# Second block's projections with the tokens' high and low parts side by side in one 512-column product

## The chip, the cores and the metric

One core of one Trainium2 chip runs the kernel. The metric is the device time of an execution in microseconds (us): the median of several runs, 1727.61 us for the kernel before (three runs, 1727.26 to 1727.88). The engines are TensorE (PE, with its weight loads as PEld), VectorE (DVE), ScalarE (ACT), GpSimd (POOL) and SyncE (SP), which issues the DMAs.

## The reference, cut to what matters

Two transformer blocks run one after the other on 256 tokens of width 1024 in float32; the first one has a mixture of experts. The change touches only the second:

```python
def second_block(x, ...):
    h = x + 0.5 * swiglu(rmsnorm(x, ffn1_norm), w_gate1, w_up1, w_down1)      # D_FF = 2816
    n = rmsnorm(h, mix_norm)
    z = n @ w_in                                                              # 1024 -> 2560
    q, k, v = z[..., :512], z[..., 512:1024], z[..., 1024:1536]
    attn = moba_attention(q, k, v)
    zg = gelu(z[..., 1536:])
    gm = chunked_spatial_gating(zg[..., :512], zg[..., 512:], ...)
    gates = sigmoid(n @ w_gate + b_gate)                                      # 1024 -> 2048
    merged = gates[..., :1024] * (attn @ w_branch_attn) + gates[..., 1024:] * (gm @ w_branch_gmlp)
    h = h + merged @ w_out
    h = h + 0.5 * swiglu(rmsnorm(h, ffn2_norm), w_gate2, w_up2, w_down2)
    return rmsnorm(h, final_norm)

def swiglu(x, w_gate, w_up, w_down):
    return (silu(x @ w_gate) * (x @ w_up)) @ w_down
```

## The kernel before

Activations lie transposed: 128 features on the partitions, the T = 256 tokens along the free axis, KD = 8 such chunks for the width of 1024. To reach float32 precision, every operand of a projection is split into a high part (a copy rounded to fp32r, made by ScalarE) and a low part (the rest, a subtraction by VectorE). `mm3` (L307 to L312) then issues three products per chunk k of the contracted width: high weights by high tokens, high weights by low tokens, low weights by high tokens, each a matmul of 128 x 128 weights with 256 token columns, all summed in one half of a PSUM bank. `xn.pair` is the pair of token tiles (`nhi`, `nlo`) that class `Normed` (L494 on) fills.

The weights come in "units" of 128 x 1024 (class `Units`): `uh` is the high part (ScalarE, L434), `ul` the low part (VectorE, L448). A unit is used by one group of 24 matmuls. `U.get(i)` emits the low part of unit i + 2 first (AHEAD = 2) and the high part of one more, so the `ul` instructions stand in VectorE's queue where the code asks for units. The program's order on each engine is the order in which the code issues; an engine runs its queue in that order.

The second block has these stages, named by their PSUM tile:

- **gu and dn** of the first FFN: `swiglu` runs over f = 0 to 21 (128 of the 2816 hidden features each). Per f it issues a gate group and an up group (8 chunks, 24 matmuls each) into the two halves of one bank; then VectorE multiplies the bank by the row scale `rs` (L1145), and `act` goes on with sigmoid (ScalarE), two multiplications (L1149, L1152) and the split (L302, L303). The down product of an earlier f (`dn`, L405, 24 matmuls of 256 columns) follows. L1199 and L509 at the end make the new residual `x` and the normed `nlo`.
- **z**: 10 column blocks j of w_in in two groups each. When `rs` is known, the groups' bank is read: q is copied by ScalarE, k is scaled by VectorE, v is copied by ScalarE (`values2`, tile `vt2`) and turned by TensorE, the rest goes through `gelu2`.
- **gt**: the gates, 8 blocks of two groups; between the groups stand steps of the attention and of the spatial gating (`pipe.tick`). VectorE scales (L1931), ScalarE takes a tanh (L1934). The attention's last step (`PT`, `pvo`) closes the stage.
- **br**: 8 chunks c; per c two groups of 4 chunks k with `ath`/`atl` and `gmh`/`gml` as tokens into two halves of one bank. `merged` combines them with the gates: L1946 (a scalar_tensor_tensor that reads the bank), L1947, a copy by ScalarE into `mgh`, and L1951 for `mgl`.
- **o**: 8 groups with `mgh`/`mgl`; one scalar_tensor_tensor per group adds the result to the residual.
- **gu and dn** of the second FFN, as before, but its down products (L2005) hold tokens as the stationary side and stream 512 columns of weights.

The working tiles in PSUM come from pool `psV` (four banks, `wps`).

Of the kernel before, what the change touches and what calls it, by code (L numbers as in the profile page):

```python
# [20 lines left out]
T = 256  # L21
# [25 lines left out]
def body(ctx: ExitStack, tc: tile.TileContext, I, out, dbg=None, n_experts=NE):  # L47
# [258 lines left out]
    def mm3(ps, wl, xl, nk, first=True, k0=0):  # L306
        (wh, wo), (xh, xo) = wl, xl  # L307
        for k in range(nk):
            for a, b in ((wh(k), xh[:, k0 + k, :]), (wh(k), xo[:, k0 + k, :]), (wo(k), xh[:, k0 + k, :])):
                nc.tensor.matmul(ps, a, b, start=first, stop=False, skip_group_check=True)  # L310
                first = False

    def rsqrt(pool, v, n, name):

        h = pool.tile([128, n], I32, name=name + "h", tag=name + "h", bufs=1)
        y = pool.tile([128, n], F32, name=name, tag=name, bufs=2)
        a = pool.tile([128, n], F32, name=name + "a", tag=name + "a", bufs=1)
# [175 lines left out]
    class Normed:  # L493


        def __init__(self, pool, x, gain):
            self.x, self.gain = x, gain
            self.hi = pool.tile([128, KD, T], F32R, name="nhi", tag="nhi", bufs=1)
            self.lo = pool.tile([128, KD, T], F32R, name="nlo", tag="nlo", bufs=1)
            self.pair = (self.hi, self.lo)  # L500

# [630 lines left out]
    def swiglu(F, n, xn, seq, down, each=None, y=None):  # L1132


        sp = {}
        gups = {}
        st = Stats(B, acc) if y is None else Rstd(B, acc, y)
        rs = None

        def act(f, halves=((0, 2),)):  # L1140
            gu = F.tile([128, 2, T], F32, name="gu", tag="gu", bufs=2)
            s = F.tile([128, T], F32, name="fs", tag="fs", bufs=2)
            for a0, a1 in halves:
                p = gups[f][a0][:, a0 * T:a1 * T].rearrange("p (a t) -> p a t", t=T)
                nc.vector.tensor_tensor(gu[:, a0:a1, :], p,  # L1145
                                        rs[:, None, :].to_broadcast([128, a1 - a0, T]), op=OP.mult)
                if a0 == 0:
                    nc.scalar.activation(s, gu[:, 0, :], AF.Sigmoid)  # L1148
                    nc.vector.tensor_tensor(s, gu[:, 0, :], s, op=OP.mult)  # L1149
                if a1 == 1:  # L1150
                    yield
# [4 lines left out]
        for kind, f in seq:  # L1156
            if kind == "gu":
                last = f == NF - 1
                gups[f] = [wps("gu")] * 2
                if last:  # L1160
                    gups[f] = gups[f][0], wps("gu")
                mm3(gups[f][0][:, 0:T], pair(U.get(order[("g", n, f)])), xn.pair, KD)
                if f == 0 and y is None:
# [607 lines left out]
    with ExitStack() as mx:  # L1771
        Q = mx.enter_context(tc.tile_pool(name="mix2", bufs=1, side="right"))
        ath = Q.tile([128, 4, T], F32R, name="ath")
        atl = Q.tile([128, 4, T], F32R, name="atl")
        gmh = Q.tile([128, 4, T], F32R, name="gmh")
        gml = Q.tile([128, 4, T], F32R, name="gml")

# [34 lines left out]

        def gelu2(ps, rs, dst, j):

            z = W3.tile([128, 2, T], F32, name="z", tag="z", bufs=2)
            t = W3.tile([128, 2, T], F32, name="ge", tag="ge", bufs=2)
            nc.vector.tensor_tensor(z, ps, rs[:, None, :].to_broadcast([128, 2, T]), op=OP.mult)
            nc.scalar.activation(t, z, AF.Square)
# [9 lines left out]

        def values2(ps, dst):
            d = W3.tile([128, 2, T], F32, name="vt2", tag="vt2", bufs=1)  # L1830
            nc.scalar.activation(d, ps, AF.Copy)
            yield
            yield from turned(d, dst, st.r.y)
# [50 lines left out]
        for n, j in enumerate(IN2):  # L1884
            ps = wps("z2")
            for a in range(2):
                mm3(ps[:, a * T:(a + 1) * T], pair(U.get(order[("in2", j, a)])), xn.pair, KD, first=(a == 0))
                pipe.tick()
# [8 lines left out]
                elif 2 * n + a == 2:  # L1897
# [3 lines left out]
                    nc.gpsimd.dma_start(ws, I["gmlp_w_s_2"][0].rearrange("g i j -> i g j"))  # L1901
            held.append((j, ps.rearrange("p (a t) -> p a t", a=2)))
            while rs is not None and held:
                k, z = held.pop(0)
                i = 2 * (k % 2)
                if k < 2:
                    nc.scalar.activation(q2[:, i:i + 2, :], z, AF.Copy)
                elif k < 4:
                    nc.vector.tensor_tensor(k2[:, i:i + 2, :], z, rs[:, None, :].to_broadcast([128, 2, T]), op=OP.mult)
                elif k < 6:  # L1910
                    pipe.start(values2(z, v2[:, :, i * 128:(i + 2) * 128]))
                else:
                    pipe.start(gelu2(z, rs, None if k < 8 else vg[:, :, i * 128:(i + 2) * 128], i))
# [6 lines left out]
        for j in range(8):  # L1920
            ps = wps("gt")
            for a in range(2):
                mm3(ps[:, a * T:(a + 1) * T], pair(U.get(order[("gate", j, a)])), xn.pair, KD, first=(a == 0))
                pipe.tick()
# [3 lines left out]
                if c in (2, 5, 8, 11):  # L1928
                    pipe.start(A.step(c // 3))
            g = gts[:, 2 * j % 8:2 * j % 8 + 2, j // 4, :]  # L1930
            nc.vector.tensor_tensor(g, ps.rearrange("p (a t) -> p a t", a=2), rs[:, None, :].to_broadcast([128, 2, T]),  # L1931
                                    op=OP.mult)
# [7 lines left out]
        W = mx.enter_context(tc.tile_pool(name="mix2d", bufs=1, side="right"))  # L1940
        mgh = W.tile([128, KD, T], F32R, name="mgh")
        mgl = W.tile([128, KD, T], F32R, name="mgl")

        def merged(c, ps):
            g = gts[:, c]
            nc.vector.scalar_tensor_tensor(g, g, 1.0, ps.rearrange("p (a t) -> p a t", a=2), op0=OP.add, op1=OP.mult)  # L1946
            nc.vector.tensor_tensor(g[:, 0, :], g[:, 0, :], g[:, 1, :], op=OP.add)  # L1947
# [5 lines left out]
        for j in range(2):  # L1953
            for a in range(2):
                ua, ug = (U.get(order[(s, j, a)]) for s in ("ba", "bg"))
                for o in range(2):
                    ps = wps("br")
                    mm3(ps[:, 0:T], pair(ua, 256, o * 128), (ath, atl), 4)
                    mm3(ps[:, T:2 * T], pair(ug, 256, o * 128), (gmh, gml), 4, first=False)
                    pipe.tick()  # L1960
# [126 lines left out]
```

## Time and profile before

| | us |
|---|---|
| median of three runs | 1727.61 |
| the profiled execution | 1726.06 |
| its span in the trace | 1724.3 |
| TensorE busy | 1606.3 |
| VectorE busy | 679.9 |
| ScalarE busy | 520.0 |
| second block, first FFN's first group to the end | about 1159 to 1724.3 |

The span is the time from the first to the last instruction of the profiled execution; the execution itself is 1.76 us longer. Busy times are the sum of an engine's instructions with overlaps taken out. A matmul's own duration in the trace (0.28 us for 256 columns) is longer than its step, the time from its start to the next one's, since matmuls overlap; where TensorE runs without a stop, the step is the time that counts, and it is read from a stretch of the chain or of the timeline divided by its matmuls.

### The profile page before, as it was taken

Reading aid. Unit: us, or ns where it says so; the run is one execution under the profiler, and the core shown is the slowest. Engines: PE = TensorE matmul, PEld = TensorE weight load, DVE = VectorE, ACT = ScalarE, POOL = GpSimd, SP = SyncE. Lnnn points to the kernel's source line nnn. Section 1 sums busy time; section 2 is a strip of 40 time slices with the busy share of each in tenths; the row PEclk is TensorE's granted clock in tenths of the full one; section 3 lists DMA queues with packets and bytes.
Section 4 is the critical chain, followed back from the end, with each engine's and each line's share of the span. In section 5 each row is a group of like instructions: output and inputs, shape, how many; then the busy total and the mean of one; then the engine's idle time right before and its main releaser. Section 6 shows DMA issues by size and latency. Waiting matters only on the chain. (4 is left out here: it accounts for less than half of the span.)

```text
span 1724.3 us, 25602 instructions
## 1 busy us (share of the span) xinstructions
PE 1606.3 (93%) x10067; PEld 982.3 (57%) x10067; DVE 679.9 (39%) x1428; ACT 520.0 (30%) x983; POOL 21.9 (1%) x39
## 2 busy tenths in 40 slices
PE   6999899999999799999999889879999999999997
PEld 3776333333333233333333233249999999999997
DVE  4656412122121212212121212146666765666666
ACT  2544312111011101201111111044444547554443
POOL 1000000000000000000000000100000000000000
PEclk7999999999999999999999999989999999999999
DMA  9987899899999999999999999965555653545652
GB/s 329 357 284 297 348 415 414 328 414 413 417 413 415 413 413 416 415 416 415 413 416 412 413 415 411 415 244 181 178 189 178 201 171 123 165 159 178 197 170 98
DMA packets 169756, 545.69 MB, mean 316 GB/s; under 512 B 11281, under 2 KB 90721, under 8 KB 133729
## 3 DMA queue, kind: packets, MB, share of 16 engines
q1 hardware_dynamic: 168304, 540.60, 81.6%
q8 instruction: 130, 2.13, 0.5%
q0 software_dynamic: 480, 1.58, 0.3%
q10 hardware_dynamic: 784, 0.92, 0.2%
q14 instruction: 58, 0.47, 0.1%
HBM read 542.01 MB, written 1.05 MB: 315 GB/s over the span
## 5 line engine op out<-in xcount | busy, mean ns | idle before, releaser
L1597 PE MATMUL u<-chunk,xg 128*64 128x512 f32 x2048 | 475.8, 604 | 16.7 <-DMA chunk<-in_w_mlp_dram 13.9
L1597 PEld LDWEIGHTS u<-chunk,xg 128*64 128x64 f32 x2048 | 152.7, 138 | 275.9 <-issue 235.6
L448 DVE TENSOR_TENSOR ul<-chunk,uh 128x1024 fp32r<-128x1024 f32 x202 | 239.2, 1220 | 36.3 <-ACT uh L434 34.9
L1499 PE MATMUL yp<-chunk,aT 128*64 128x512 f32 x1024 | 235.8, 602 | 9.5 <-ACT aT L1484 8.1
L434 ACT ACTIVATE uh<-chunk 128x1024 fp32r<-128x1024 f32 x202 | 205.1, 1050 | 58.4 <-DMA chunk<-in_ffn_w_up_dram 24.1
L310 PE MATMUL gu<-nhi,uh 128*128 128x256 f32 x704 | 200.0, 284 | 0.0
L310 PE MATMUL gu<-nhi,ul 128*128 128x256 f32 x704 | 199.4, 283 | 0.0
L310 PE MATMUL gu<-nlo,uh 128*128 128x256 f32 x704 | 199.4, 283 | 0.0
L1499 PEld LDWEIGHTS yp<-chunk,aT 128*64 128x64 f32 x1024 | 68.0, 137 | 128.3 <-issue 113.8
L310 PEld LDWEIGHTS gu<-nhi,uh 128*128 128x128 f32 x704 | 135.3, 192 | 1.2 <-issue 0.4
L310 PEld LDWEIGHTS gu<-nlo,uh 128*128 128x128 f32 x704 | 135.3, 192 | 0.9
L310 PEld LDWEIGHTS gu<-nhi,ul 128*128 128x128 f32 x704 | 135.3, 192 | 0.0
L1474 DVE TENSOR_SCALAR g<-u 128x256 f32<-128x256 f32 x64 | 27.1, 423 | 226.3 <-PE u L1597 222.9
L1509 DVE SCALAR_TENSOR_TENSOR yl<-yp,tg,yh 128x512 fp32r<-128x512 f32 x32 | 24.0, 751 | 222.9 <-ACTq L1627 172.2
L1475 ACT ACTIVATE s<-g 128x256 f32<-128x256 f32 x66 | 27.2, 413 | 234.8 <-DVE g L1474 232.2
L1508 ACT ACTIVATE yh<-yp,tg 128x512 fp32r<-128x512 f32 x32 | 22.0, 687 | 165.4 <-PEq L1696 148.7
L1484 ACT ACTIVATE aT<-apt 128x256 f32<-128x256 f32 x64 | 24.5, 383 | 141.6 <-PE apt L297 74.2
L1253 ACT ACTIVATE xr<-xrp,yg 128x512 f32<-128x512 f32 x32 | 22.0, 688 | 146.3 <-PE xrp L1242 146.3
L1145 DVE TENSOR_TENSOR gu<-gu,rs 128x512 f32<-128x512 f32 (+1 forms) x46 | 30.7, 668 | 80.7 <-PE gu L310 80.2
L1271 DVE TENSOR_TENSOR xg<-xrp,gs 128x128 f32<-128x128 f32 x64 | 18.7, 292 | 106.8 <-ACT xg L1266 106.8
L1266 ACT ACTIVATE xg<-xrp,modT,gs 128x64 f32<-128x64 f32 x128 | 44.8, 400 | 51.2 <-PE xrp L1260 39.7
L1148 ACT ACTIVATE fs<-gu 128x256 f32<-128x256 f32 x44 | 18.4, 418 | 122.9 <-DVE gu L1145 122.9
(472 smaller groups left out, 2362.8 us busy)
## 6 DMA issues: line engine op xcount, KB each, us to landing
chunk<-in_w_mlp_dram SPq DMA_DIRECT2D x384, 1024.0 KB, 19.9
chunk<-in_w_ada_dram SPq DMA_DIRECT2D x24, 1024.0 KB, 7.3
chunk<-in_ffn_w_gate_dram SPq DMA_DIRECT2D x22, 1024.0 KB, 5.6
chunk<-in_ffn_w_up_dram SPq DMA_DIRECT2D x22, 1024.0 KB, 8.0
chunk<-in_ffn_w_down_dram SPq DMA_DIRECT2D x22, 1024.0 KB, 5.8
chunk<-in_w_in_dram SPq DMA_DIRECT2D x17, 1024.0 KB, 5.2
chunk<-in_w_gate_dram SPq DMA_DIRECT2D x8, 1024.0 KB, 5.4
chunk<-in_w_out_dram SPq DMA_DIRECT2D x6, 1024.0 KB, 8.0
```

What stands on the lines that cost most here:

```text
L310: nc.tensor.matmul(ps, a, b, start=first, stop=False, skip_group_check=True)
L434: nc.scalar.activation(hi if spec is None else spec(hi), view(raw(key)), AF.Copy)
L448: nc.vector.tensor_tensor(vl, view(raw(key)), vh.bitcast(F32), op=OP.subtract)
L1145: nc.vector.tensor_tensor(gu[:, a0:a1, :], p, rs[:, None, :].to_broadcast([128, a1 - a0, T]), op=OP.mult)
L1253: nc.scalar.activation(xr[q][0:w, :], ps[1 + q][0:w, :], AF.Copy, scale=ps[0][0:w, :])
L1266: nc.scalar.activation(xg[:, k, :], at, AF.Identity, scale=gs[:, 2, k:k + 1], bias=modT[:, 24 + k:25 + k])
L1474: nc.vector.tensor_scalar(g, uv[:, :, 0], 7.0, None, op0=OP.min)
L1475: nc.scalar.activation(s, g, AF.Sigmoid, scale=1.702)
L1484: nc.scalar.activation(aT[:, r * 256:(r + 1) * 256], pt[:, r * 256:(r + 1) * 256], AF.Copy)
L1499: nc.tensor.matmul(yp[w * d:w * d + w, 0:m], a, wt[:, o:o + m], start=(q + h == 0), stop=(q + h == 4), skip_group_check=True, tile_positio ...
L1509: nc.vector.scalar_tensor_tensor(yl, yp[:, 0:m], tg[:, 1:2], yh.bitcast(F32), op0=OP.mult, op1=OP.subtract)
L1597: nc.tensor.matmul(u, xg[j][:, k, :], raw(("m1", e, k))[:, n * 512:(n + 1) * 512], start=False, stop=(k == KD - 1), skip_group_check=True, ...
```

## The change

A helper `wide3` takes the place of `mm3` in all projections of the second block except the down products. Per chunk k it issues two matmuls instead of three: the high weights with 512 columns (256 high and 256 low tokens, which now lie side by side in one tile), and the low weights with the 256 high tokens. The 512 columns fill a whole PSUM bank, whose halves have to be added: `summed` is a VectorE tensor_reduce over pairs (256 outputs from 512 inputs whose partners lie 256 elements apart). Each group now takes a bank of its own, and the steps that read PSUM before read the summed tile in SBUF. In o the two halves are added by two scalar_tensor_tensor. The ScalarE copies of q and v out of PSUM fall away, as the sums write q2 and `vt2` themselves.

```diff
+    def wide3(ps, wl, both, nk, first=True):
+        wh, wo = wl
+        for k in range(nk):
+            nc.tensor.matmul(ps, wh(k), both[:, k], start=first, stop=False, skip_group_check=True)
+            nc.tensor.matmul(ps[:, 0:T], wo(k), both[:, k, 0, :], start=False, stop=False, skip_group_check=True)
+            first = False
+    def summed(dst, ps):
+        nc.vector.tensor_reduce(dst, ps.rearrange("p (s t) -> p t s", s=2), axis=AX.X, op=OP.add)
...
-            self.hi = pool.tile([128, KD, T], F32R, name="nhi", tag="nhi", bufs=1)
-            self.lo = pool.tile([128, KD, T], F32R, name="nlo", tag="nlo", bufs=1)
-            self.pair = (self.hi, self.lo)
+            self.both = pool.tile([128, KD, 2, T], F32R, name="nboth", tag="nboth", bufs=1)
+            self.hi, self.lo = self.both[:, :, 0, :], self.both[:, :, 1, :]
...
-                gups[f] = [wps("gu")] * 2
-                if last:
-                    gups[f] = gups[f][0], wps("gu")
-                mm3(gups[f][0][:, 0:T], pair(U.get(order[("g", n, f)])), xn.pair, KD)
+                gus[f] = F.tile([128, 2, T], F32, name="gu", tag="gu", bufs=2)
+                ps = [wps("gu") for _ in range(2)]
+                wide3(ps[0], pair(U.get(order[("g", n, f)])), xn.both, KD)
+                summed(gus[f][:, 0, :], ps[0])
...
-                mm3(gups[f][1][:, T:2 * T], pair(U.get(order[("u", n, f)])), xn.pair, KD, first=last)
+                wide3(ps[1], pair(U.get(order[("u", n, f)])), xn.both, KD)
+                summed(gus[f][:, 1, :], ps[1])
...
-        def values2(ps, dst):
-            d = W3.tile([128, 2, T], F32, name="vt2", tag="vt2", bufs=1)
-            nc.scalar.activation(d, ps, AF.Copy)
+        def values2(d, dst):
...
-            ps = wps("z2")
+            i = 2 * (j % 2)
+            if j < 4:
+                z = (q2, k2)[j // 2][:, i:i + 2, :]
+            else:
+                z = W3.tile([128, 2, T], F32, name="z", tag="vt2" if j < 6 else "z", bufs=1 if j < 6 else 2)
             for a in range(2):
-                mm3(ps[:, a * T:(a + 1) * T], pair(U.get(order[("in2", j, a)])), xn.pair, KD, first=(a == 0))
+                ps = wps("z2")
+                wide3(ps, pair(U.get(order[("in2", j, a)])), xn.both, KD)
+                summed(z[:, a, :], ps)
...
-            ps = wps("gt")
+            g = gts[:, 2 * j % 8:2 * j % 8 + 2, j // 4, :]
             for a in range(2):
-                mm3(ps[:, a * T:(a + 1) * T], pair(U.get(order[("gate", j, a)])), xn.pair, KD, first=(a == 0))
+                ps = wps("gt")
+                wide3(ps, pair(U.get(order[("gate", j, a)])), xn.both, KD)
+                summed(g[:, a, :], ps)
...
+            t = W.tile([128, 2, T], F32, name="brs", tag="brs", bufs=2)
+            for a in range(2):
+                summed(t[:, a, :], ps[a])
+            nc.vector.scalar_tensor_tensor(g, g, 1.0, t, op0=OP.add, op1=OP.mult)
...
-                    ps = wps("br")
-                    mm3(ps[:, 0:T], pair(ua, 256, o * 128), (ath, atl), 4)
-                    mm3(ps[:, T:2 * T], pair(ug, 256, o * 128), (gmh, gml), 4, first=False)
+                    ps = [wps("br") for _ in range(2)]
+                    wide3(ps[0], pair(ua, 256, o * 128), atb, 4)
+                    wide3(ps[1], pair(ug, 256, o * 128), gmb, 4)
...
-                mm3(ps[:, :T], pair(U.get(order[("out2", j, a)])), (mgh, mgl), KD)
-                nc.vector.scalar_tensor_tensor(x4[:, c, :], ps[:, :T], 0.5, x3[:, c, :], op0=OP.mult, op1=OP.add)
+                wide3(ps, pair(U.get(order[("out2", j, a)])), mgb, KD)
+                for p, x in ((ps[:, 0:T], x3), (ps[:, T:2 * T], x4)):
+                    nc.vector.scalar_tensor_tensor(x4[:, c, :], p, 0.5, x[:, c, :], op0=OP.mult, op1=OP.add)
```

The scheduling is that of the code, so what moves is VectorE's queue. In the middle of the first FFN, VectorE's rows for one f before (operation, output<-inputs, size; L1145 is the multiplication by `rs`):

```order
L1145 TENSOR_TENSOR gu<-gu,rs 128x512
L1149 TENSOR_TENSOR fs<-gu,fs 128x256
L1152 TENSOR_TENSOR fs<-gu,fs 128x256
L303 TENSOR_TENSOR spl<-fs,sph 128x256
L448 TENSOR_TENSOR ul<-chunk,uh 128x1024 x3
```

And now (L324 is the sum, L461 the low part of a unit, L1156 the multiplication):

```order
L324 TENSOR_REDUCE gu<-gu 128x256
L461 TENSOR_TENSOR ul<-chunk,uh 128x1024
L324 TENSOR_REDUCE gu<-gu 128x256
L1156 TENSOR_TENSOR gu<-gu,rs 128x512
L1160 TENSOR_TENSOR fs<-gu,fs 128x256
L1163 TENSOR_TENSOR fs<-gu,fs 128x256
L303 TENSOR_TENSOR spl<-fs,sph 128x256
L461 TENSOR_TENSOR ul<-chunk,uh 128x1024 x2
```

A sum of the gate group stands between two low parts of units, and a sum of the up group ahead of the multiplication; VectorE meets two waits for TensorE per f instead of one.

In the br stage, VectorE's rows before from a pair of low parts on (L1946, L1947 and L1951 are `merged`):

```order
L448 TENSOR_TENSOR ul<-chunk,uh 128x1024 x2
L1951 TENSOR_TENSOR mgl<-gts,mgh 128x256
L1946 SCALAR_TENSOR_TENSOR gts<-gts,br 128x512
L1947 TENSOR_TENSOR gts<-gts 128x256
L1951 TENSOR_TENSOR mgl<-gts,mgh 128x256
L1946 SCALAR_TENSOR_TENSOR gts<-gts,br 128x512
L1947 TENSOR_TENSOR gts<-gts 128x256
```

And now the same stretch (L1963, L1964 and L1968 are `merged`):

```order
L461 TENSOR_TENSOR ul<-chunk,uh 128x1024 x2
L1968 TENSOR_TENSOR mgb<-gts,mgb 128x256
L324 TENSOR_REDUCE brs<-br 128x256 x2
L1963 SCALAR_TENSOR_TENSOR gts<-gts,brs 128x512
L1964 TENSOR_TENSOR gts<-gts 128x256
L1968 TENSOR_TENSOR mgb<-gts,mgb 128x256
L324 TENSOR_REDUCE brs<-br 128x256 x2
L1963 SCALAR_TENSOR_TENSOR gts<-gts,brs 128x512
L1964 TENSOR_TENSOR gts<-gts 128x256
```

Each L1946 has got two sums ahead of it, so twelve entries stand where eight stood.

## Rows read from the trace of the kernel before

**Rows 1.** The page, busy times of the whole span.

```profile
PE 1606.3 (93%) x10067; PEld 982.3 (57%) x10067; DVE 679.9 (39%) x1428; ACT 520.0 (30%) x983; POOL 21.9 (1%) x39
```

**Rows 2.** Windows by stage: length, busy us (xinstructions) per engine, PEclk, DMA share, GB/s.

```profile
1176.00:1344.00 168.00, 168.00 (x1400) 168.00 (x1401) 105.99 (x139) 72.71 (x99) 0.00 (x0) 1.00 0.58 189
1355.00:1414.00 59.00, 59.00 (x496) 58.41 (x493) 42.03 (x71) 28.40 (x41) 2.03 (x2) 1.00 0.58 181
1414.00:1478.00 64.00, 62.56 (x529) 56.78 (x528) 33.03 (x58) 44.68 (x103) 0.00 (x0) 1.00 0.37 122
1478.00:1500.30 22.30, 22.30 (x197) 22.13 (x196) 18.95 (x29) 10.68 (x16) 0.00 (x0) 1.00 0.62 193
1500.30:1522.00 21.70, 21.70 (x194) 21.70 (x193) 16.19 (x25) 11.61 (x16) 0.00 (x0) 1.00 0.59 191
```

**Rows 3.** Chain of waits, second block: start, us, engine, tile, line, xinstructions.

```profile
1387.36 23.03 PE z L310 x192
...
1478.33 21.98 PE br L310 x192
1500.32 21.76 PE o L310 x192
...
1566.68 5.74 PE gu L310 x48
1572.41 2.80 PE dn L2005 x12
```

**Rows 4.** Timeline of TensorE in the first block's y stage: start, us, work.

```profile
147.06 0.62 PE L1039 MATMUL y<-u,mixh 128*128 128x512 f32 x2
147.51 0.39 PE L1039 MATMUL y<-u,mixl 128*128 128x512 f32 x1
147.74 0.62 PE L1039 MATMUL y<-u,mixh 128*128 128x512 f32 x2
...
150.46 0.62 PE L1039 MATMUL y<-u,mixh 128*128 128x512 f32 x2
```

**Rows 5.** VectorE groups by form: out<-in, xcount, busy, mean ns, idle before.

```profile
L1474 DVE TENSOR_SCALAR g<-u 128x256 f32<-128x256 f32 x64 | 27.1, 423 | 226.3 <-PE u L1597 222.9 <-DVEq L1678 3.0
...
L565 DVE TENSOR_REDUCE attst<-sc 128x1 f32<-128x256 f32 x16 | 6.6, 415 | 0.0
...
L935 DVE TENSOR_REDUCE ss<-scr 128x4 f32<-128x512 f32 x2 | 1.4, 682 | 0.0
...
L1447 DVE TENSOR_REDUCE gt<-og 128x32 f32<-128x128 f32 x2 | 0.7, 374 | 0.1
```

**Rows 6.** Timeline of VectorE, one f of the first FFN.

```profile
1265.28 0.69 DVE L1145 TENSOR_TENSOR gu<-gu,rs 128x512 f32<-128x512 f32 x1 [2.26 <-PE gu L310]
1266.45 0.43 DVE L1149 TENSOR_TENSOR fs<-gu,fs 128x256 f32<-128x256 f32 x1 [0.48 <-ACT fs L1148]
...
1268.16 3.49 DVE L448 TENSOR_TENSOR ul<-chunk,uh 128x1024 fp32r<-128x1024 f32 x3
1273.91 0.69 DVE L1145 TENSOR_TENSOR gu<-gu,rs 128x512 f32<-128x512 f32 x1 [2.27 <-PE gu L310]
```

**Rows 7.** Timeline of VectorE in the br stage.

```profile
1485.10 2.36 DVE L448 TENSOR_TENSOR ul<-chunk,uh 128x1024 fp32r<-128x1024 f32 x2
1487.37 0.42 DVE L1951 TENSOR_TENSOR mgl<-gts,mgh 128x256 fp32r<-128x256 f32 x1
1487.71 0.68 DVE L1946 SCALAR_TENSOR_TENSOR gts<-gts,br 128x512 f32<-128x512 f32 x1
1488.42 0.43 DVE L1947 TENSOR_TENSOR gts<-gts 128x256 f32<-128x256 f32 x1
1488.76 0.42 DVE L1951 TENSOR_TENSOR mgl<-gts,mgh 128x256 fp32r<-128x256 f32 x1
```

**Rows 8.** Windows of the in2 projections.

```profile
1386.90:1398.60 11.70, 11.70 (x101) 11.70 (x99) 9.10 (x24) 3.73 (x5) 1.09 (x1) 1.00 0.33 98
1398.60:1410.60 12.00, 12.00 (x103) 12.00 (x102) 11.57 (x15) 7.55 (x9) 0.00 (x0) 1.00 0.68 210
```

**Rows 9.** Timeline of TensorE at the first down product.

```profile
1175.94 0.39 PE L405 MATMUL dn<-sph,ul 128*128 128x256 f32 x1 [0.88 <-DVE ul L448]
```

**Rows 10.** Chain of waits at the ends of the first FFN and of gt.

```profile
1344.83 2.27 DVE ul L448 x2
1347.10 1.20 DVE x L1199 x2
...
1475.03 0.70 DVE gts L1931
```

More of the change, by code (lines that the diff above doesn't have):

```diff
@@ L1135, in swiglu @@
         sp = {}
-        gups = {}
+        gus = {}
         st = Stats(B, acc) if y is None else Rstd(B, acc, y)
@@ L1140, in act @@
         def act(f, halves=((0, 2),)):
-            gu = F.tile([128, 2, T], F32, name="gu", tag="gu", bufs=2)
+            gu = gus[f]
             s = F.tile([128, T], F32, name="fs", tag="fs", bufs=2)
             for a0, a1 in halves:
-                p = gups[f][a0][:, a0 * T:a1 * T].rearrange("p (a t) -> p a t", t=T)
-                nc.vector.tensor_tensor(gu[:, a0:a1, :], p,
+                nc.vector.tensor_tensor(gu[:, a0:a1, :], gu[:, a0:a1, :],
                                         rs[:, None, :].to_broadcast([128, a1 - a0, T]), op=OP.mult)
@@ L1772, in body @@
         Q = mx.enter_context(tc.tile_pool(name="mix2", bufs=1, side="right"))
[L1773 to L1776, printed above, removed]
+        atb = Q.tile([128, 4, 2, T], F32R, name="atb")
+        ath, atl = atb[:, :, 0, :], atb[:, :, 1, :]
+        gmb = Q.tile([128, 4, 2, T], F32R, name="gmb")
+        gmh, gml = gmb[:, :, 0, :], gmb[:, :, 1, :]
         gts = Q.tile([128, KD, 2, T], F32, name="gts")
@@ L1811, in turned, with gelu2 @@
                         nc.scalar.activation(d[:, b, :], pt[:, b * 128:(b + 1) * 128], AF.Copy, scale=scale[:, b:b + 1])
-        def gelu2(ps, rs, dst, j):
-            z = W3.tile([128, 2, T], F32, name="z", tag="z", bufs=2)
+        def gelu2(z, rs, dst, j):
             t = W3.tile([128, 2, T], F32, name="ge", tag="ge", bufs=2)
-            nc.vector.tensor_tensor(z, ps, rs[:, None, :].to_broadcast([128, 2, T]), op=OP.mult)
+            nc.vector.tensor_tensor(z, z, rs[:, None, :].to_broadcast([128, 2, T]), op=OP.mult)
             nc.scalar.activation(t, z, AF.Square)
@@ L1901, in body @@
                     nc.gpsimd.dma_start(ws, I["gmlp_w_s_2"][0].rearrange("g i j -> i g j"))
-            held.append((j, ps.rearrange("p (a t) -> p a t", a=2)))
+            held.append((j, z))
             while rs is not None and held:
@@ L1905, in body @@
                 i = 2 * (k % 2)
[L1906 to L1910, printed above, removed]
+                if 2 <= k < 4:
+                    nc.vector.tensor_tensor(z, z, rs[:, None, :].to_broadcast([128, 2, T]), op=OP.mult)
+                elif 4 <= k < 6:
                     pipe.start(values2(z, v2[:, :, i * 128:(i + 2) * 128]))
-                else:
+                elif k >= 6:
                     pipe.start(gelu2(z, rs, None if k < 8 else vg[:, :, i * 128:(i + 2) * 128], i))
@@ L1929, in body @@
                     pipe.start(A.step(c // 3))
-            g = gts[:, 2 * j % 8:2 * j % 8 + 2, j // 4, :]
-            nc.vector.tensor_tensor(g, ps.rearrange("p (a t) -> p a t", a=2), rs[:, None, :].to_broadcast([128, 2, T]),
+            nc.vector.tensor_tensor(g, g, rs[:, None, :].to_broadcast([128, 2, T]),
                                     op=OP.mult)
@@ L1940, in body @@
         W = mx.enter_context(tc.tile_pool(name="mix2d", bufs=1, side="right"))
-        mgh = W.tile([128, KD, T], F32R, name="mgh")
-        mgl = W.tile([128, KD, T], F32R, name="mgl")
+        mgb = W.tile([128, KD, 2, T], F32R, name="mgb")
+        mgh, mgl = mgb[:, :, 0, :], mgb[:, :, 1, :]
         def merged(c, ps):
             g = gts[:, c]
-            nc.vector.scalar_tensor_tensor(g, g, 1.0, ps.rearrange("p (a t) -> p a t", a=2), op0=OP.add, op1=OP.mult)
+            t = W.tile([128, 2, T], F32, name="brs", tag="brs", bufs=2)
+            for a in range(2):
+                summed(t[:, a, :], ps[a])
+            nc.vector.scalar_tensor_tensor(g, g, 1.0, t, op0=OP.add, op1=OP.mult)
             nc.vector.tensor_tensor(g[:, 0, :], g[:, 0, :], g[:, 1, :], op=OP.add)
```

## The prediction

> **What bounds the kernel now.** I read the page's busy times first: TensorE works 93% of the span, VectorE 39% [rows 1]. [...] The change takes columns' overhead from TensorE and gives VectorE 140 sums (88 in the FFNs, 20 in z, 16 in gt, 16 in br), so the question is where VectorE can't carry them.
>
> **TensorE's part.** The chain gives steps where TensorE never stops. Per matmul of 256 columns: z 23.03/192 = 120.0 ns, gu 5.74/48 = 119.6, which I round to 120, o 21.76/192 = 113.3 [rows 3]. The same shape costs two prices, by the tiles it reads. For 512 columns with 128 x 128 weights there are two prices as well: in y 15 matmuls start between 147.06 and 150.46, 3.40/15 = 226.7 ns [rows 4]; dn of the second FFN takes 2.80/12 = 233.3 [rows 3]. A k costs now 3 x 120 = 360 in gu, z and gt, and 3 x 113.3 = 340 in br and o. After: one of 512 and one of 256. The cheap 512 goes with the dear 256 as a pattern: 226.7 is 106.7 above 120, so 512 columns bear the same overhead of 13.3 as 256 do, and I pair 226.7 + 120 = 346.7 for gu, z and gt, where the moving and the stationary tiles stay what they were. That saves 13.3 ns per k. For br and o I pair 233.3 + 113.3 = 346.7, 6.7 ns more than now. Bounds: 233.3 + 120 = 353.3 (saves 6.7) and 226.7 + 113.3 = 340 (saves 20).
>
> The k's are 22 x 2 x 8 x 2 = 704 in the FFNs, 160 in z, 128 in gt, 64 in br and 64 in o. Of gu's, 48 at the start of the first FFN lie beside waits of their own and save nothing. 944 x 13.3 ns = **-12.6 us**; o adds 64 x 6.7 ns = +0.4.
>
> **What a sum costs.** No row shows a reduce over pairs out of PSUM. A plain one takes 415 ns for 256 inputs and 682 for 512 [rows 5], 1.04 ns per input, whatever leaves it. At that rate a sum is 0.68 us, 0.65 from start to start. Two things could add to it: partners 256 elements apart, and 256 outputs. Reading PSUM in steps costs nothing where the trace has it: 128x256 taken from every second element of u takes 423 [rows 5], about the 415 of a plain reduce of as many. The reduce that steps by 32 elements in SBUF, four inputs to an output, takes 374 for 128 inputs [rows 5]; half of what lies between 415 and 682 taken off 415 is 281 for 128, so it pays 93 ns more: 0.7 per input or 2.9 per output. Carried over, a sum would be 0.68 + 512 x 0.7 = 1.04 us, or 0.68 + 256 x 2.9 = 1.42. I take 0.68, since the u row reads PSUM as the sum does, and keep 1.04 and 1.42 as the ends.
>
> [...]
>
> **Where the sums are hidden, and where not.** *The FFNs.* One f lasts 1273.91 - 1265.28 = 8.63 us, of which VectorE waits 2.27 for gu, so it works 6.37 [rows 6] (less its short waits for ScalarE, which don't move). Two sums make it 7.7. TensorE's f becomes 8.64 less 16 x 13.3 ns = 8.43: the sums fit, and cost nothing while a sum stays below 1.03. PSUM doesn't stop it: four banks hold two f's, and a sum follows its group at once.
> *Start of the first FFN.* TensorE already waits 0.88 us for a `ul` at the first down product [rows 9]; sums now stand in that queue ahead of it. Two sums ahead of it, less the little slack, are +1.2, and one more at the next unit some +0.75 (estimates from 0.65 a sum): **+2.0**.
> *End of the first FFN.* The chain runs over VectorE there: ul 2.27, then x 1.20 [rows 10]. The last up group's sum stands ahead, and the gate's beside: +0.65 to +1.3, I take **+1.1**.
> *z.* From 1386.9 to 1410.6 VectorE works 9.10 of 11.7 and then 11.57 of 12.0 [rows 8]: 3.0 us idle, and eight groups' sums want 5.2. So it falls 2.2 behind, 3.1 with the 0.85 that TensorE would gain there. What it owes are units' low parts, which TensorE needs. I take **+2.6**.
> *gt.* VectorE has half its time [rows 2]. Only the last sum lies on the chain into L1931 at 1475.03 [rows 10]: **+0.7**.
> *br.* Per c VectorE does half a pair of low parts, 2.27/2, then 0.34, 0.71 and 0.34 from start to start [rows 7], 2.53 together, and about 2.56 with its small gaps; TensorE's c is 24 x 114.5 ns = 2.75 [rows 3]. Two sums make VectorE's 3.9. Eight c's are 31, from a queue that starts on the first sum some 3.1 us into the stage (a `ul` pair stands ahead, as before). I walked its queue by the order of the change: the last mgb comes 32.0 us into br, and out2's first group, whose last k needs it, ends at 32.45. Before it ended at 21.98 + 21.76/8 = 24.7. **+7.7**, the largest loss; the stage's balance gives about the same, 18.95 + 16 x 0.65 = 29.4 of work in 22.3.
> *o.* Eight more operations of 0.42 [rows 7] in a stage with 21.70 - 16.19 = 5.5 idle [rows 2]: hidden. *The second FFN's* start waits for its statistics on TensorE itself, and at its end down products are held back that cover the last sums: nothing. Two ScalarE copies each for q and v fall away, off every chain: nothing.
>
> **The sum.** -12.6 + 0.4 + 2.0 + 1.1 + 2.6 + 0.7 + 7.7 = +1.9 us on the profiled execution of 1726.06, whose span is 1724.3. It lies 1.55 below the median of 1727.61; the same difference on the median gives **1729.5**. The terms of VectorE carry some 4 us of doubt: 1726 to 1734.
>
> **Rivals.** *A, the stepping read costs.* VectorE then sets the pace in more than br. At 1.04 us a sum an FFN's f needs 6.37 + 2.08 = 8.45, just what TensorE takes, while br loses 16 x 0.36 = 5.8 more, z 20 x 0.36 = 7.2 and the ends 1.5: 1729.5 + 14.5 = 1744. At 1.42 each f takes 9.2 instead of 8.43, 41 x 0.77 = 32 on top, and br, z and the ends twice what they lose at 1.04: 1729.5 + 32 + 29 = 1790. It decides from 1.03 us on. For it: the 374 row. Against it: the u row.
> *B, the 512 columns cost 233.3 in gu too.* The saving halves: 944 x 6.7 = 6.3, so 1735.8, slower. For it: dn in this same block takes that. Against: its `ul` and `sp` tiles aren't those of gu.
> *C, the pair costs less, and the change is faster.* At 340 ns the saving is 944 x 20 = 18.9 us, +0.4 - 0.4 for o, and 1722.8 comes out; if both matmuls got o's overhead of 6.7, 220 + 113.3, it would be 944 x 26.7 = 25.2 and 1716.5. For it: the layout of the tiles changes, and o shows that layout is worth 6.7 ns a matmul [rows 3]. Against: the token tile of gu keeps its weights beside it.
> [...]
>
> **How the numbers follow.** The chances: my forecast 0.45, A 0.27 (0.15 at about 1.04, 0.12 above), B 0.10, C 0.18. A change below 0.2%, 3.5 us, can't be told from none. The forecast's own range 1726 to 1734 lies mostly within it: of its 0.45, 0.30 count as same, 0.12 as slower and 0.03 as faster. A and B are slower, C faster for 0.15 of its 0.18. Together faster 0.18, same 0.33, slower 0.49. The range leaves out A's upper end and the far end of C: 1718 to 1750.
>
> **What would show it.** In the changed trace: a gu stretch of 32 matmuls at 173.3 ns on average (5.55 us per f); the sum's row at 0.68; in br, TensorE idle for VectorE and VectorE busy without a gap, out2's start some 8 us later; in the middle of an FFN, TensorE without idle time. Sums of 1 us or more with TensorE waiting in each f would show A; gu at 353 per k B, at 340 or less C. I would be wrong in the balance if br's low parts went elsewhere in time, or if VectorE's queue were late in gt, where I count nothing.

## The result, and the profile after

The changed kernel takes 1739.8 us (median of four runs, 1738.99 to 1741.05), the kernel before beside it 1727.74 us. The ratio of the runs is 1.0074, 95% interval 1.0062 to 1.0086; the two medians differ by 12.1 us. The profiled execution's span is 1737.3 us. The time lies inside the prediction's range of 1718 to 1750 us, 10 us above its forecast of 1729.5.

The page of the changed kernel, to be held against [rows 1]:

```profile
PE 1606.0 (92%) x8947; PEld 927.2 (53%) x8947; DVE 770.8 (44%) x1576; ACT 517.5 (30%) x979; POOL 21.9 (1%) x39
```

TensorE's busy time has hardly moved, VectorE's has grown by 90.9 us, with 148 instructions more: the 140 sums, and 8 second additions in o. The windows by stage (length, busy us of PE, PEld, DVE, ACT and POOL, then PEclk) answer to [rows 2]; the stages have moved by the time lost:

```profile
1176.00:1344.00 168.00, 167.00 (x1103) 152.59 (x1104) 131.85 (x180) 73.12 (x98) 0.00 (x0) 1.00 0.58 188
1349.20:1415.10 65.90, 63.41 (x365) 52.52 (x365) 55.71 (x101) 32.70 (x48) 3.10 (x5) 1.00 0.52 161
1415.10:1480.20 65.10, 62.81 (x407) 50.38 (x405) 45.66 (x78) 43.32 (x101) 0.00 (x0) 0.99 0.41 135
1480.20:1507.80 27.60, 24.17 (x129) 20.52 (x129) 25.94 (x40) 10.49 (x15) 0.00 (x0) 0.96 0.47 153
1507.80:1535.00 27.20, 25.00 (x129) 21.00 (x130) 22.31 (x38) 12.02 (x17) 0.00 (x0) 0.94 0.48 155
```

VectorE fills br now, 25.94 of 27.6 us, and TensorE, which was busy without a stop there, idles for 3.4 us; PEclk is below 1.00 in gt, br and o.

Of each stage, from its first matmul to the next stage's in the two timelines ("third down" is the third group of down products, and so on; the prediction's column has its terms put into these stretches):

| stretch | before us | after us | change | as predicted |
|---|---|---|---|---|
| first FFN, first gu to third down | 40.48 | 43.38 | +2.9 | +1.6 |
| its middle, 15 f's | 129.60 | 127.90 | -1.7 | -3.2 |
| its end, to the first z | 23.04 | 24.27 | +1.2 | +0.7 |
| z | 64.85 | 65.83 | +1.0 | +0.5 |
| gt | 64.82 | 65.11 | +0.3 | -1.0 |
| br and o | 43.65 | 54.79 | +11.1 | +8.1 |
| second FFN, first gu to fourth down | 50.34 | 51.54 | +1.2 | -1.3 |
| its middle, 14 f's | 119.56 | 116.95 | -2.6 | -3.0 |
| its end | 32.53 | 33.82 | +1.3 | -0.4 |

The first gu matmul starts at 1155.47 us in the trace of before and at 1153.68 in that of after. The stretches add up to +14.7, the spans differ by 13.0 and the medians by 12.1: the profiled execution of before came late out of the first block (its first x2t matmul starts at 1152.17, that of after at 1150.39; in all kernels below it lies between 1150.1 and 1153.2). The first FFN's start is not longer for that: e1 below, whose first x2t matmul starts at 1152.01, takes 43.29 us there, and e6, with 1151.75, takes 40.07.

The sum itself, in VectorE's groups by form (out<-in, count, busy us, mean ns):

```profile
L324 DVE TENSOR_REDUCE gu<-gu 128x256 f32<-128x512 f32 x88 | 60.3, 686 | 30.2 <-PE gu L319 30.1
...
L324 DVE TENSOR_REDUCE gts<-gt 128x256 f32<-128x512 f32 x16 | 11.0, 689 | 12.7 <-PE gt L319 12.6
L324 DVE TENSOR_REDUCE brs<-br 128x256 f32<-128x512 f32 x16 | 10.4, 682 | 0.8 <-PE br L319 0.8
```

It takes 682 to 689 ns, as the plain reduce of 512 inputs in [rows 5], with partners 256 elements apart and 256 outputs.

One f of the first FFN on VectorE's timeline, beside [rows 6]:

```profile
1265.47 0.69 DVE L324 TENSOR_REDUCE gu<-gu 128x256 f32<-128x512 f32 x1 [0.82 <-PE gu L319]
1266.20 0.69 DVE L1156 TENSOR_TENSOR gu<-gu,rs 128x512 f32<-128x512 f32 x1
...
1269.10 2.35 DVE L461 TENSOR_TENSOR ul<-chunk,uh 128x1024 fp32r<-128x1024 f32 x2
1271.37 0.68 DVE L324 TENSOR_REDUCE gu<-gu 128x256 f32<-128x512 f32 x1
1271.97 1.22 DVE L461 TENSOR_TENSOR ul<-chunk,uh 128x1024 fp32r<-128x1024 f32 x1
1274.00 0.69 DVE L324 TENSOR_REDUCE gu<-gu 128x256 f32<-128x512 f32 x1 [0.82 <-PE gu L319]
```

Two sums fit between the low parts; VectorE still waits for TensorE, 0.82 us per f, so in the middle of the FFN the sums cost nothing. TensorE's chain there, two neighbouring f's of each FFN (the start of the down products):

```profile
1265.44 2.88 PE dn L418 x24
1273.96 2.87 PE dn L418 x24
...
1611.71 2.80 PE dn L2023 x12
1620.07 2.80 PE dn L2023 x12
```

One f lasts 8.52 us in the first FFN and 8.36 in the second, against 8.64 and 8.54 before. With the down product taken off and by 16 k's that is 353 ns per k in the first FFN and 347 in the second.

### The profile page after: what moved, and what is told of

Same layout as the page of the kernel before. It is cut to its first block, busy times and chain, and to the rows that moved or that the text cites. A ratio compares the mean times of both kernels' runs of the same rounds, so it can differ in the third digit from the quotient of the medians.

```text
span 1737.3 us, 23544 instructions
## 1 busy us (share of the span) xinstructions
PE 1606.0 (92%) x8947; PEld 927.2 (53%) x8947; DVE 770.8 (44%) x1576; ACT 517.5 (30%) x979; POOL 21.9 (1%) x39
## 5 line engine op out<-in xcount | busy, mean ns | idle before, releaser
L1609 PE MATMUL u<-chunk,xg 128*64 128x512 f32 x2048 | 475.3, 604 | 15.4 <-DMA chunk<-in_w_mlp_dram 12.7
L461 DVE TENSOR_TENSOR ul<-chunk,uh 128x1024 fp32r<-128x1024 f32 x202 | 242.2, 1218 | 25.3 <-ACT uh L447 25.3
L318 PE MATMUL gu<-nboth,uh 128*128 128x512 f32 x704 | 249.5, 396 | 0.0
L319 PE MATMUL gu<-nboth,ul 128*128 128x256 f32 x704 | 197.9, 281 | 3.0 <-DVE ul L461 3.0
L318 PEld LDWEIGHTS gu<-nboth,uh 128*128 128x128 f32 x704 | 132.4, 188 | 30.2 <-issue 0.4
L1511 PEld LDWEIGHTS yp<-chunk,aT 128*64 128x64 f32 x1024 | 68.1, 137 | 128.3 <-issue 114.5
L319 PEld LDWEIGHTS gu<-nboth,ul 128*128 128x128 f32 x704 | 133.2, 189 | 5.2 <-DVE ul L461 4.3
L324 DVE TENSOR_REDUCE gu<-gu 128x256 f32<-128x512 f32 x88 | 60.3, 686 | 30.2 <-PE gu L319 30.1
L318 PE MATMUL z<-nboth,uh 128*128 128x512 f32 x160 | 58.1, 404 | 1.7 <-DVE nboth L521 1.7
```

Source lines behind the costliest of these rows:

```text
L318: nc.tensor.matmul(ps, wh(k), both[:, k], start=first, stop=False, skip_group_check=True)
L319: nc.tensor.matmul(ps[:, 0:T], wo(k), both[:, k, 0, :], start=False, stop=False, skip_group_check=True)
L324: nc.vector.tensor_reduce(dst, ps.rearrange("p (s t) -> p t s", s=2), axis=AX.X, op=OP.add)
L461: nc.vector.tensor_tensor(vl, view(raw(key)), vh.bitcast(F32), op=OP.subtract)
L1511: nc.tensor.matmul(yp[w * d:w * d + w, 0:m], a, wt[:, o:o + m], start=(q + h == 0), stop=(q + h == 4), skip_group_check=True, tile_positio ...
L1609: nc.tensor.matmul(u, xg[j][:, k, :], raw(("m1", e, k))[:, n * 512:(n + 1) * 512], start=False, stop=(k == KD - 1), skip_group_check=True, ...
```

## Experiments

The ratios are those of the runs of each kernel to runs of the kernel before on the same chip; they can differ in the last digit from the quotient of the two medians.

**br and o as before (e1_br_o_old).**

```diff
...
-                    ps = [wps("br") for _ in range(2)]
-                    wide3(ps[0], pair(ua, 256, o * 128), atb, 4)
-                    wide3(ps[1], pair(ug, 256, o * 128), gmb, 4)
+                    ps = wps("br")
+                    mm3(ps[:, 0:T], pair(ua, 256, o * 128), (ath, atl), 4)
+                    mm3(ps[:, T:2 * T], pair(ug, 256, o * 128), (gmh, gml), 4, first=False)
...
-                wide3(ps, pair(U.get(order[("out2", j, a)])), mgb, KD)
+                mm3(ps[:, :T], pair(U.get(order[("out2", j, a)])), (mgh, mgl), KD)
...
```

> The br and o stages go back to three products of 256 columns; FFNs, z and gt stay changed. Theory (VectorE's sums in br hold TensorE, and the idle time drops its clock): br and o together fall from 54.8 us to the 43.7 of before, no half-clock stretch at the start of o, and 1728.7 us in all (1727.5 to 1730.5). Rival (the loss is spread over the stages by dearer 512-column matmuls): these two stages give back no more than their matmuls, 128 k's x 13 ns = 1.7 us, so 1738.

Measured 1729.23 us against 1726.92, ratio 1.0011 (1.0001 to 1.0020). Of the 12 us, 9.8 are gone: br and o carry the loss, and what the other stages gain and lose nearly cancels. br and o take 45.25 us here, though, 1.6 more than before. The windows of the first 3.4 us of br and of the rest of br and o (PEclk is the figure after POOL's) say why:

```profile
1481.40:1484.80 3.40, 3.40 (x18) 3.40 (x18) 2.69 (x3) 2.27 (x3) 0.00 (x0) 0.53 0.03 9
1484.80:1526.60 41.80, 41.80 (x369) 41.80 (x369) 32.52 (x51) 20.00 (x29) 0.00 (x0) 1.00 0.61 201
```

TensorE starts br at a granted clock of 0.53, and its first 18 matmuls take about 189 ns each (3.40/18), where the 369 behind them take 113 (41.80/369). Before this it stood still for `PT`, for 2.3 us as in the changed kernel: that wait lies at the end of gt, where a sum still stands on the chain.

**Only the FFNs (e2_ffn_only).** z, gt, br and o go back to `mm3`.

> Only the two FFNs stay changed; z, gt, br and o are as before. Theory: the middle of the FFNs saves 4.4 us (2.0 in the first, 2.4 in the second) and the four ends lose about 4.9 to sums on the chain, so 1728 us, within 0.2% of before. Rival (the ends' loss comes from elsewhere, the FFN itself gains what its matmuls save): 1723 us.

Measured 1728.74 us, ratio 1.0010 (1.0000 to 1.0019): the middle of the FFNs saves 127.90 - 129.60 = -1.7 and 116.94 - 119.56 = -2.6 us, and their starts and ends lose it again (43.27 for 40.48, 23.76 for 23.04, 51.22 for 50.34, 33.81 for 32.53). Alone, the FFN's part of the change is worth nothing, or a little less.

**Half the sum (e3_half_sum).** The low tokens' half of each product with the high weights is left out of the result.

```diff
-        nc.vector.tensor_reduce(dst, ps.rearrange("p (s t) -> p t s", s=2), axis=AX.X, op=OP.add)
+        nc.vector.tensor_copy(dst, ps[:, 0:T])
```

> The sum is replaced by a copy of one half of the bank (256 inputs in place of 512), so the high weights' product with the low tokens' half is computed but left out of the result. A copy is expected at 0.42 us, 0.34 from start to start, against 0.60 of the sum. Theory (VectorE's time per sum is what is lost): br gives back 16 x 0.26 = 4.2 us and the ends and z some 3 us, 1732.5 (1730 to 1735). Rival (the wait for a sum, its place in the queue, matters and not its length): above 1737.

Measured 1730.42 us against 1726.92, ratio 1.0019 (1.0010 to 1.0029). The copy takes 422 ns in place of 686, and TensorE's matmuls are the same: the loss falls from 12 to 3.5 us. The matmuls and the bank that each group takes are those of the changed kernel, so most of the loss is VectorE's time per sum, and neither TensorE's steps nor the doubled use of banks. br and o still take 51.72, 8.1 more than before: the two copies per c, 0.42 us each, are VectorE's time too.

**The wide products first (e4_order).**

```diff
         for k in range(nk):
             nc.tensor.matmul(ps, wh(k), both[:, k], start=first, stop=False, skip_group_check=True)
+            first = False
+        for k in range(nk):
             nc.tensor.matmul(ps[:, 0:T], wo(k), both[:, k, 0, :], start=False, stop=False, skip_group_check=True)
-            first = False
```

> Within each group all 512-column products are issued first, then all 256-column ones, instead of alternating. If the 353 ns per k of the first FFN comes from alternating two widths, a k falls to 226.7 + 120 = 346.7 there, in z and in gt, worth about 3 us, and the low parts of the weights are needed half a group later, worth 1 to 3 us at the FFNs' starts and in z: 1735 us. If a step depends on the width alone, only the latter: 1738.

Measured 1739.23 us, ratio 1.0068 (1.0052 to 1.0085): no change that can be told. The middle of the first FFN goes from 127.90 to 127.00, so (127.00/15 - 2.88)/16 = 349 ns per k: the alternation accounts for a part of the 353, short of the 346.7. The middle of the second FFN goes the other way, from 116.95 to 117.23, or (117.23/14 - 2.80)/16 = 348 ns. In this order the two FFNs, at 353 and 347 in the changed kernel, differ by 1 ns, so most of their difference goes with the alternation. The first FFN's start takes longer, 44.95.

**TensorE kept busy in its waits (e5_keep_busy).**

```diff
+    def keep(n, both, d=None):
+        d = acc("dm") if d is None else d
+        for i in range(n):
+            nc.tensor.matmul(d, both[:, 0, 0, 0:128], both[:, 0], start=True, stop=False, skip_group_check=True)
...
+            if at == k:
+                keep(10, atb_[0])
...
+        keep(8, xn.both)
...
+        atb_.append(atb)
+        keep(9, atb)
...
-                wide3(ps, pair(U.get(order[("out2", j, a)])), mgb, KD)
+                wide3(ps, pair(U.get(order[("out2", j, a)])), mgb, KD, at=6 if c == 0 else None)
```

The first `keep` stands in `wide3`, ahead of the product of chunk k; the 8 follow gt's last group and the 9 br's last.

> The changed kernel with 27 extra 512-column products whose result nobody reads, put where TensorE waits: 8 after the last gt group, 9 after the last br group, 10 ahead of the seventh k of o's first group. Theory (the waits drop TensorE's clock to its lower level for some 3 us after gt and again after br): both half-clock stretches go, o's first groups take 1.8 us less and br's start up to 1.5 us less, of which VectorE's backlog hides a half: 10 us above before in place of 12. Rival (the waits alone cost, the clock comes back in their shadow): no gain, or up to 1 us slower where an extra product stands in the way.

Measured 1737.62 us against 1726.60, ratio 1.0071 (1.0054 to 1.0087); against the 1.0074 of the changed kernel the intervals don't tell them apart. The windows do. First the changed kernel: the start of br, the wait ahead of o with its next stretch, and the rest of o.

```profile
1479.50:1482.30 2.80, 2.80 (x10) 2.08 (x9) 1.62 (x3) 2.03 (x3) 0.00 (x0) 0.50 0.00 0
1505.80:1513.20 7.40, 3.44 (x17) 2.14 (x15) 7.12 (x14) 1.36 (x3) 0.00 (x0) 1.00 0.45 143
1513.20:1516.80 3.60, 3.60 (x12) 3.05 (x12) 2.95 (x4) 1.88 (x3) 0.00 (x0) 0.53 0.00 0
1516.80:1535.00 18.20, 18.20 (x105) 15.82 (x104) 14.25 (x24) 8.78 (x12) 0.00 (x0) 1.00 0.53 174
```

In 7.4 us TensorE was busy for 3.44, and then ran 3.6 us at 0.53; br's first 2.8 us ran at 0.50. With the extra products, the same places and one in the middle of br:

```profile
1479.80:1482.50 2.70, 2.70 (x16) 2.37 (x16) 2.16 (x3) 2.28 (x3) 0.00 (x0) 1.00 0.00 0
1499.50:1502.80 3.30, 3.30 (x12) 2.75 (x11) 3.20 (x6) 2.26 (x3) 0.00 (x0) 0.50 1.01 308
1508.20:1512.00 3.80, 3.80 (x21) 3.19 (x20) 3.58 (x9) 1.44 (x3) 0.00 (x0) 1.00 0.48 167
1512.00:1533.00 21.00, 21.00 (x119) 18.19 (x118) 17.23 (x28) 10.61 (x15) 0.00 (x0) 1.00 0.46 151
```

Both places are at 1.00, o takes 24.92 us instead of 27.13; but br now has a drop in its middle, to 0.50 over 3.30 us after a wait of 1.84 us for a bank, and takes 28.39 instead of 27.66. In sum br and o are 1.5 us shorter. So at the two places the clock stays up where TensorE is kept busy; the gain of 2 us that the theory forecast is not shown, as a drop came elsewhere.

**The middle of the FFNs alone (e6_ffn_middle).** As e2_ffn_only, with `mm3` and the old reading of the bank where f is 0, 1, 2 or 21.

> Only the FFNs are changed, and in them f = 0, 1, 2 and 21 keep three products of 256 columns; z, gt, br and o as before. Theory (inside the FFN the sums are hidden, and the ends where they are not ate the gain): 18 f's times 0.11 us in the first FFN and 0.19 in the second, 5.4 us faster than before: ratio 0.997. Rival (sums cost in the middle as well, or TensorE's gain is smaller than read): as with whole FFNs, within 1 us of e2_ffn_only.

Measured 1720.62 us against 1726.60, ratio 0.9966 (0.9955 to 0.9978): faster, and by what was expected. The FFNs' starts and ends are back at what they were or below (40.07, 22.92, 49.88, 32.39), their middles unchanged at 127.90 and 116.95. So in e2_ffn_only the ends lost what the middles gained.

**ScalarE shares the sum (e8_act_helps).**

```diff
-        nc.vector.tensor_reduce(dst, ps.rearrange("p (s t) -> p t s", s=2), axis=AX.X, op=OP.add)
+        low = B.tile([128, T], F32, name="hs", tag="hs", bufs=2)
+        nc.scalar.activation(low, ps[:, T:2 * T], AF.Copy)
+        nc.vector.tensor_tensor(dst, ps[:, 0:T], low, op=OP.add)
```

> The changed kernel, but a sum is a ScalarE copy of the low half into SBUF and a VectorE addition of the high half to it: VectorE's share falls from 0.60 to some 0.34 us, ScalarE gets 140 copies of 0.4. Theory (VectorE's time is the bound in br and z): br gives back 4 us, and the ends lose the copy's latency, 0.4 us each: 4 to 6 us above before. Rival (ScalarE's queue or the handover between the engines takes its place): 9 us or more above before.

Measured 1742.10 us, ratio 1.0093 (1.0076 to 1.0110): the rival is right. VectorE's part is 423 ns, and br and o fall to 51.6, but z takes 68.0 and gt 67.5 us, 2.2 and 2.4 more than in the changed kernel, and the starts of the FFNs take 44.1 and 52.7, 0.7 and 1.2 more. The windows of z and gt of this kernel (ACT is the fourth busy time):

```profile
1351.30:1419.30 68.00, 63.75 (x365) 52.53 (x365) 51.15 (x101) 37.23 (x64) 3.11 (x5) 1.00 0.49 157
1419.30:1486.80 67.50, 64.71 (x408) 50.72 (x405) 40.51 (x78) 49.84 (x121) 0.00 (x0) 0.99 0.40 129
```

ScalarE does much of the attention's work in gt, 49.84 of 67.5 us now; a copy stands in its queue among that work, and VectorE's addition behind the copy. That the queue is what costs is argued from this, not tried apart.

**z and gt (e7_middle_gt, e9_middle_gt_no_z).** e7_middle_gt is e6_ffn_middle with z changed and gt but for j = 7; e9_middle_gt_no_z leaves z as before.

> e6_ffn_middle with z changed as well, and gt but for its last block j = 7. Theory: z loses 1.0 us (VectorE was full there), gt gains 14 groups times 8 x 9.5 ns = 1.1 us once its last sums are off the chain and the clock drop at br's start is gone: the same as e6_ffn_middle within 0.5 us. Rival (gt's loss was not its last sums): 2 us slower than e6_ffn_middle.

> The FFNs changed but for f = 0, 1, 2 and 21, gt changed but for j = 7, and z, br and o as before. From the stages of the earlier runs: 18 f's x (0.11 + 0.19) = 5.4 us in the FFNs and 1.0 us in gt, nothing lost in z: 6.4 us faster than before, ratio 0.9963; if br and o run at 118 ns a matmul as in e6_ffn_middle instead of 113 as before, 1.7 us less of that.

Measured: e7 1721.03 us against 1726.60, ratio 0.9970 (0.9960 to 0.9979); e9 1719.48 against 1727.69, ratio 0.9958 (0.9944 to 0.9971). z takes 65.75 us in e7, where it is changed, and 64.86 in e9; gt takes 63.84 and 63.88 in place of 64.82. With the last block's sums off the chain, gt gains its matmuls' 1.0 us and br takes 21.88 us, where the kernel before has 21.89 and a granted clock of 1.00 [rows 2]. Both came out as expected from the stages (e7 within 0.5 us of e6, e9 at 0.9963). e9 is faster than the kernel before by its own comparison; against e6 and e7 it is not told apart.

**The program of e6_ffn_middle again (e10_again), and another order of the down products (e11_down_order).**

> e6_ffn_middle once more. Its br and o took 118 ns per matmul of 256 columns, where before and e2_ffn_only, with the same code and addresses there, took 113. If that is set by what runs before on TensorE in this program, it comes again: br and o 45.3 us together. If it is set anew in every execution, it may be 43.7.

In the chain of e6_ffn_middle the br and o stages read:

```profile
1475.72 22.81 PE br L310 x192
1498.53 22.61 PE o L310 x192
```

and in that of the repeated one:

```profile
1474.26 21.98 PE br L310 x192
1496.25 21.76 PE o L310 x192
```

That is 118.8 and 114.5 ns per matmul in br (22.81/192, 21.98/192), 117.8 and 113.3 in o; the repeated one took 1718.77 us, in one execution. The program is the same, so what runs before on TensorE does not set the step alone. The chip is not the same (15 for e6, 3 for e10), but e7 took the lower step in the same stages (43.64 us for both) on chip 15. That the step is set anew in every execution fits this; it was not tried by repeats on one chip. Between two profiled executions, up to 1.7 us of br and o can be this.

> e9_middle_gt_no_z with the three products of the first FFN's down step in another order (high weights by high tokens, low weights by high tokens, high weights by low tokens); no other matmul changes. If the 353 ns per k of the first FFN (347 in the second) hangs on the sequence of matmuls around it, its 15 f's of 8.527 us change, by up to 1.6 us in all; if on the tiles that are read, they stay at 127.90.

Measured 1720.69 us against 1727.69, ratio 0.9961 (0.9945 to 0.9976); the first FFN's 15 f's take 127.90 again. The order of the down products doesn't set it. What was expected for this case, that the tiles read do, is left over but not shown: no run moved them.

## Why the prediction was right or wrong

**The direction given the best chance and the br mechanism were right; the sum was short by 10 us.** The forecast was +1.9, with slower the likeliest of the three at 0.49; measured are +12.1. The time lies above the forecast's own 1726 to 1734, in a part of the range that rivals had opened: A, with dearer sums, did not occur, and B accounts for some 2.5 us. That the range holds the time is therefore in good part luck. By the stretches of the table, 12.7 us more were lost than predicted: 6.0 at the FFNs' starts and ends, 3.0 in br and o, 1.9 in the FFNs' middles, 1.3 in gt and 0.5 in z.

**The sum's price** was right: 0.68 predicted, 686 ns measured, and rival A with its dearer sums did not occur. That the sums fit into the middle of an FFN was right as well, with 0.82 us of VectorE to spare per f.

**br** was the right place and mechanism. VectorE's queue in the changed kernel:

```profile
1484.39 0.69 DVE L324 TENSOR_REDUCE brs<-br 128x256 f32<-128x512 f32 x1 [0.42 <-PE br L319]
...
1487.22 0.69 DVE L324 TENSOR_REDUCE brs<-br 128x256 f32<-128x512 f32 x1 [0.35 <-PE br L319]
...
1489.02 2.35 DVE L461 TENSOR_TENSOR ul<-chunk,uh 128x1024 fp32r<-128x1024 f32 x2
1491.29 0.42 DVE L1968 TENSOR_TENSOR mgb<-gts,mgb 128x256 fp32r<-128x256 f32 x1
1491.62 1.28 DVE L324 TENSOR_REDUCE brs<-br 128x256 f32<-128x512 f32 x2
1492.93 0.69 DVE L1963 SCALAR_TENSOR_TENSOR gts<-gts,brs 128x512 f32<-128x512 f32 x1
1493.66 0.43 DVE L1964 TENSOR_TENSOR gts<-gts 128x256 f32<-128x256 f32 x1
1494.00 0.42 DVE L1968 TENSOR_TENSOR mgb<-gts,mgb 128x256 fp32r<-128x256 f32 x1
1494.34 1.28 DVE L324 TENSOR_REDUCE brs<-br 128x256 f32<-128x512 f32 x2
1495.65 0.69 DVE L1963 SCALAR_TENSOR_TENSOR gts<-gts,brs 128x512 f32<-128x512 f32 x1
1496.38 0.43 DVE L1964 TENSOR_TENSOR gts<-gts 128x256 f32<-128x256 f32 x1
1496.72 2.35 DVE L461 TENSOR_TENSOR ul<-chunk,uh 128x1024 fp32r<-128x1024 f32 x2
```

From 1489.02 on there is no gap: a pair of low parts and two sets of sums and merges last from 1489.02 to 1496.72, 7.7 for two c's where 2 x 3.9 = 7.8 was reckoned. The walk put the last `mgb` 32.0 us into br; it ended at 32.97 (1513.13 - 1480.16). VectorE waited 0.42 and 0.35 for br's first matmuls, and these ran at a granted clock of 0.50. o's second group starts 33.68 us into br, where the walk has 32.45; the other 1.7 us that br and o lost beyond the forecast came behind that, where TensorE ran at 0.53 until 1516.8 and a k cost 353 ns and not the forecast 346.7.

**The clock is the mechanism that was not in the sum.** A wait was priced at its length. Behind two waits here the granted clock fell, to 0.50 over 2.8 us and to 0.53 over 3.6, and the matmuls slowed with it: two 512-column products of br start at 1480.97 and 1481.61, 0.64 us for a k, and two later ones at 1483.13 and 1483.49, 0.36. One such place is br's start after the wait for `PT`, which grew from 1.44 us in the kernel before (first line) to 2.29:

```profile
1477.09 0.81 PE L602 MATMUL pvo<-PT,v 128*64 128x256 f32 x3 [1.44 <-ACT PT L594]
...
1478.56 0.81 PE L614 MATMUL pvo<-PT,v 128*64 128x256 f32 x3 [2.29 <-ACT PT L606]
```

The other is o's start. With TensorE kept busy (e5), o took 27.13 - 24.92 = 2.2 us less and br 0.7 more. In e1 br, with its old matmuls and a drop at its start, took 23.49 - 21.89 = 1.6 us more than before.

**TensorE's saving** was mis-sized, 13.3 ns per k: the second FFN's middle gave 2.61 us over 14 x 16 k's, 11.7 ns, and the first FFN's 1.70 over 15 x 16, 7.1. As sums, "226.7 + 120" held in the second FFN (347) and the bound "233.3 + 120 = 353.3" in the first, in br and in o. z and gt lie between, some 350. So rival B, given 0.10, holds in the first FFN: over its middle 1.5 us, with z and gt (288 k's by 3.5 ns) 2.5. The prediction put o's 113.3 ns down to the tiles that it reads; e6 and e10, one program, took 117.8 and 113.3 ns there, so the tiles alone do not set it.

**The FFNs' starts and ends** were the largest miss. The second FFN's were put at nothing, on a reading of the chain before. In the chain of after, its end goes over two sums,

```profile
1715.68 1.14 DVE ul L461
1716.82 0.61 DVE gu L324
1717.45 0.43 DVE gu L1156
1718.85 1.14 DVE ul L461
1719.98 0.61 DVE gu L324
1720.62 0.44 DVE gu L1156
```

and TensorE waits 0.90 us for a `ul` in its start, where it did not wait before:

```profile
1563.47 0.39 PE L319 MATMUL gu<-nboth,ul 128*128 128x256 f32 x1 [0.90 <-DVE ul L461]
```

In the first FFN the wait at the first down product was 0.88 us in [rows 9]; it is 1.68 now, and `gu` groups beside it wait too (line of the waits: total, times, longest):

```profile
1176.48 0.38 PE L418 MATMUL dn<-sph,ul 128*128 128x256 f32 x1 [1.68 <-DVE ul L461]
...
PE gu L319 <- DVE ul L461: 2.1, 2, 1.6
```

The prediction had the first of these waits and not the others. The four stretches changed by +6.6 us, where +0.6 was predicted; e6, which leaves the sums out there and keeps them in the middle, has all of it back.

**z** lost 1.0 where +0.5 stood. The forecast mechanism is there, TensorE waiting for low parts that VectorE owes, and no such wait stands in the trace of before:

```profile
PE z L319 <- DVE ul L461: 1.5, 2, 1.1
```

**gt** lost 0.3 where -1.0 stood; the cause is its last block (e7 and e9 gain 1.0 there).

**What stays open:** why a k costs 353 ns in the first FFN and 347 in the second. The order of the down product does not set it (e11). The order within a group has a part in it: with the wide products first both come to 348 or 349 (e4), but why alternating should cost more in one FFN than in the other no run shows, and the addresses of the tiles were not varied. And how the ends' excess is split between the sums on the chain and the low parts behind them was not tried apart.

## What to carry to other kernels

Price an operation that moves from a busy engine to an idle one stage by stage: here the middle of the FFNs had 2.27 us of room per f and took the sums for nothing, while br, z and the starts and ends had none, and cost several times what was gained. Apply such a change where the other engine waits, and leave it out where it does not, and in the first and last rounds of a loop, where its operations lie on the chain: with the same helper in the middles of the FFNs and in gt but for its last block the kernel takes 1719.48 us (e9), against 1739.8 with it everywhere. And read the granted clock behind each wait of the matrix engine: where it has fallen, the wait costs its length and the slow stretch behind it, here 2.8 us at 0.50 and 3.6 us at 0.53.

## What the runs showed of the hardware

- After a stretch in which TensorE was busy for 3.44 of 7.4 us, and after a wait of 2.29 us, its granted clock was 0.53 and 0.50 for 3.6 and 2.8 us; after the wait of 1.44 us at the latter place in the kernel before it stayed at 1.00.
- A matmul's step was not set by its shape and its program alone here: 256 columns took 113.3 or 117.8 ns in o of two executions of one program (on two chips), and a 512- and a 256-column product together 353 or 347 ns in the first and the second FFN of one execution.
- A reduce over pairs that lie 1 KB apart in PSUM took 686 ns for 512 inputs, against 682 for the plain reduce of 512 in [rows 5].
